# Gates of the last merge with seven products of quarters instead of eight

## The chip, the cores and the metric

The kernel runs on one core of one Trainium2 chip. A core has a matrix unit (TensorE, PE in the profile; its weight loads are shown apart as PEld), three engines that work element by element (VectorE, DVE; ScalarE, ACT; GpSimd, POOL), SyncE (SP), which issues most transfers here, and 16 DMA engines that move data between DRAM and the on-chip memories. SBUF is the large on-chip memory with 128 partitions; PSUM is the small one into which TensorE sums. Each engine takes its own instructions in order and waits on semaphores for the others.

The metric is the time of one execution on the device, in microseconds (us).

## The reference

One layer of a network with three parallel branches, over 2048 sample tokens and 128 prompt tokens, 1024 channels wide, all in float32:

```python
proj = jnp.einsum('btd,de->bte', xn, w_in)            # xn: modulated RMSNorm of x
qkv, beta, dec, z_a, u_b, v_b, z_b, x_c, z_c, gates = jnp.split(proj, points, axis=-1)
# A: short convolution of qkv, gated delta rule in both directions -> o_a   (512 channels)
# B: gating by a spatial matrix in chunks of 128 tokens            -> o_b   (512)
# C: Fourier mixing over tokens and channels                       -> o_c   (512)
br = jnp.stack([o_a, o_b, o_c], axis=2)
pb = jnp.einsum('btnw,nwd->btnd', br, w_branch)       # 512 -> 1024, per branch
gt = jax.nn.sigmoid(gates.reshape(B, T, N_BRANCH, D_MODEL))
merged = jnp.einsum('btnd,btnd->btd', gt, pb)
out = jnp.einsum('btd,de->bte', merged, w_out)
# then y = rmsnorm(x + gate * out)
```

What the change touches is `gates` of branch A: a product of the normalized tokens (2176 x 1024) with 1024 columns of `w_in`, whose sigmoid multiplies branch A's projection.

## The kernel before

**Numbers.** Every float32 operand of a matmul is split into two float16 parts, a high and a low one, and a product is three matmuls: high by high, high by low, low by high. TensorE thus does 3 matmuls for each 128 channels of the inner dimension (`gemm_T`, line 162 calls `mm`, line 161). Before the split an operand is scaled by a power of two that comes from its sum of squares.

**Tiles.** The normalized tokens lie in SBUF for the whole run as two tiles `xh` and `xl` (128 partitions x 8 blocks of channels x 2176 tokens). Tokens are taken in five blocks, four of 512 and one of 128 (`TBS`). A gate row is one block of 128 output channels (`db`); for a block of 512 tokens it costs 8 x 3 = 24 matmuls of 512 columns, and the branch product, with 4 blocks of channels, costs 12.

**Weights.** All weight blocks stand in one list, `wlist`, in the order of use. Each is read by SP into one of two staging buffers (`wst`, `read_w`) and converted there by a generator, `converting`: ScalarE squares it with a running sum (line 209), VectorE casts the sum (line 175), a one-column matmul adds it over partitions, VectorE makes the power of two from it in four small operations (lines 183 to 187) and its inverse (216), ScalarE writes the high part (218), VectorE the low part (219). Conversions are pushed forward by `weight_step`, one step at a time, from inside the matmul loops (`pace.tick`); `getw(n, ahead)` hands out the next blocks and asks for those ahead.

**Stages.** Norms and the input projection of decays and gates for branch A; 12 blocks of the short convolution, each over the five token blocks, beside which the decays of the delta rule are worked out and stored (`decays`, up to about 275 us; later convolutions to 450 us); the preparation of the delta rule with branches B and C; the three merges, for B, C and A in this order (`merge`, lines 1324 to 1374), the scan of the delta rule running beside the first two; then the output projection.

**A merge** runs over 8 rows `db`; in each, over two halves of the tokens and their blocks: gate product, sigmoid with its scale (ScalarE, line 1351), branch product from `big` (branch values in high and low parts), product of the two (VectorE, 1360), addition to the row `mrow` read from DRAM (read by SP, line 1339; addition on GpSimd, 1361; store by GpSimd's queue, 1368). The last merge, for branch A (line 1461), takes the halves in reversed order. In each of its rows `tail` also reads and converts one block of 128 columns of `w_out` (`out_w`) into tiles of their own, `wohi` and `wolo`, and `gate_rows` makes the output gate. After the later tokens of the last row, `ahead_out` prepares the first five output tiles (`out_prep`: square, scale, high part at line 1428, low part); the prompt's tile comes first, then tokens 1024 to 2047, then the others.

**Order.** The instructions of each engine are put in order when the program is built: a planner simulates the engines and places the instructions by their dependences and its own costs; `tc.high_priority()` moves the ones inside ahead. A pool's `bufs` says how many tiles of a name exist, and so when the next can be written.

Of the kernel before, what the change touches and what calls it, by code (L numbers as in the profile page):

```python
# [11 lines left out]
F16 = mybir.dt.float16  # L12
# [25 lines left out]
FS = 4096.0  # L38
TBS = [(0, 512), (512, 512), (1024, 512), (1536, 512), (2048, 128)]
# [72 lines left out]
def hybrid_flow_kernel(ctx: ExitStack, tc: tile.TileContext, x_prompt, x_sample, state_delta, c, c_ctx, ln_g, w_ada,  # L112
# [85 lines left out]
    def converting(w, st, nkt, cols=P, hi=None, lo=None, tag="w", bufs=5):  # L198
# [15 lines left out]
        s, inv = scales(None, wp, "wsc", sb16)  # L214
# [12 lines left out]
    xh = sb(xnp, [P, KT, NTOK], "xh", F16)  # L227
    xl = sb(xnp, [P, KT, NTOK], "xl", F16)

    def gemm_T(ps, w, c0, rh, rl, nkt=KT, start=True, stop=True):  # L230
        for k in range(nkt):
            mm(ps, w.hi[:, k, c0:c0 + P], rh[:, k, :], start and k == 0, False)
            mm(ps, w.hi[:, k, c0:c0 + P], rl[:, k, :], False, False)
            mm(ps, w.lo[:, k, c0:c0 + P], rh[:, k, :], False, stop and k == nkt - 1)
            if k % 2:
                pace.part(rh.shape[-1] / 400)

    def gemm_N(ps, lh, ll, w, c0, n, nkt=KT):
        for k in range(nkt):
            mm(ps, lh[:, k, :], w.hi[:, k, c0:c0 + n], k == 0, False)  # L240
            mm(ps, lh[:, k, :], w.lo[:, k, c0:c0 + n], False, False)
            mm(ps, ll[:, k, :], w.hi[:, k, c0:c0 + n], False, k == nkt - 1)
# [13 lines left out]
    for n in (1, 2, 0):  # L256
        for db in range(KT):
            wlist.append((w_in_[:, C_G + n * D + db * P:C_G + n * D + (db + 1) * P], KT, "w", 4))
            wlist.append((w_branch[0, n][:, db * P:(db + 1) * P], 4, "b", 2))
# [4 lines left out]
    def read_next():  # L264
        if len(wread) < min(len(wdone) - len(wsteps) + 2, len(wlist)):
            src, nkt, tag, bufs = wlist[len(wread)]
            wread.append(read_w(src, nkt))

    def begin():

        i = len(wdone)
        if i >= goal[0] or (wlist[i][2] == "b" and not bwp):
            return False
        if len(wread) == i:
            read_next()
        wdone.append(_W())
        wsteps.append(converting(wdone[i], wread[i], wlist[i][1], tag=wlist[i][2], bufs=wlist[i][3]))
        return True

# [134 lines left out]
    with tc.high_priority():  # L414
# [6 lines left out]
        A.activation(bnd[:, 0, :], ms.rearrange("p k g -> p (k g)"), AF.Square, scale=math.sqrt(2.0 * D), accum_out=bss[:, 0:1])  # L421
        A.activation(bnd[:, 1, :], sh.rearrange("p k g -> p (k g)"), AF.Square, scale=math.sqrt(2.0), accum_out=bss[:, 1:2])
# [15 lines left out]
    for ti, (t0, tn) in enumerate(TBS):  # L438
# [13 lines left out]
        for k in range(KT):  # L452
# [5 lines left out]
            A.copy(xh[:, k, t0:t0 + tn], t)  # L458
            G.tensor_tensor(xl[:, k, t0:t0 + tn], t, xh[:, k, t0:t0 + tn], ALU.subtract)
        for g in range(4):  # L460
            ps = bank(ps_d if tn == P and g % 2 else ps_mm, [P, tn])
            gemm_T(ps, zaw[g], 0, xh[:, :, t0:t0 + tn], xl[:, :, t0:t0 + tn])
# [32 lines left out]
    def decays():  # L495
        pbs = sb(dq, [P, NCH, 16], "sq")
        for c0, c1 in ((0, 9), (9, NCH)):
            pb = bank(ps_mm, [P, c1 - c0, 32])
            for t in range(c0, c1):
                ts = slice(t * P, (t + 1) * P)  # L500
                for k in range(KT):
                    if k == KT - 1:
                        mm(pb[:, t - c0, 0:16], xl[:, k, ts], bdp[:, k, 0:16], False, False)
                    mm(pb[:, t - c0, :], xh[:, k, ts], bdp[:, k, :], k == 0, k == KT - 1)
                    if k < KT - 1:
                        mm(pb[:, t - c0, 0:16], xl[:, k, ts], bdp[:, k, 0:16], False, False)
# [74 lines left out]
        def flush(t, row):  # L581
            A.activation(row, row, AF.Exp)
            A.dma_start(decD[t], row.rearrange("p d h i -> p d (h i)"))
# [20 lines left out]
    flip = [0]  # L604
    pace.start(decays(), 1.2)
    for ct in range(12):
        w = getw(1, 2 if ct < 6 else min(4, 15 - ct))
        for half in range(1):
# [4 lines left out]
            for t0, tn in TBS:  # L613
                flip[0] ^= 1
                ps = bank(ps_d if flip[0] else ps_mm, [P, tn])
                gemm_T(ps, w, 0, xh[:, :, t0:t0 + tn], xl[:, :, t0:t0 + tn])
# [17 lines left out]
    pace.drain()  # L634
    a1.close()
# [467 lines left out]
    def silu_unit(ti, w):  # L1103
        t0, tn = TBS[ti]
        ps = bank(ps_mm, [P, tn])
        gemm_T(ps, w, 0, xh[:, :, t0:t0 + tn], xl[:, :, t0:t0 + tn])
# [48 lines left out]
    for t in range(NCH):  # L1155
        ps = bank(ps_mm, [P, 4, P])
        ts = slice(t * P, (t + 1) * P)
# [370 lines left out]
```

## Time and profile before

| | us |
|---|---|
| median of 3 runs | 2205.78 (2198.61 to 2207.93) |
| the profiled execution | 2208.47, of which the span is 2206.7 |
| TensorE busy | 2138.4 (97% of the span) |
| VectorE / ScalarE / GpSimd busy | 1299.4 / 1005.0 / 708.8 |
| later convolutions | 275 to 450 |
| delta preparation, branches B and C | 450 to 1084 |
| merge B, merge C | 1084 to 1417.9, 1417.9 to 1750.0 |
| merge A (the last) | 1750.0 to 2018.5 |
| output projection | 2018.5 to 2206.7 |

In the views of the profile a line such as `L161 PE MATMUL b<-xh,whi` names the line of the kernel, the engine, the operation, the tile written and those read; x and a number are how many; min/median/max and means of one instruction are in nanoseconds, starts in us from the start of the span. What stands in brackets behind `<-` is what ended the idle time of the engine just before. A helper's line stands for all its callers, so the tile's name tells which it is. Matmuls overlap in TensorE: one of 512 columns is shown as 0.38 us long, but the next one starts 0.216 us later, and the spacing is what counts.

### The profile page before, as it was taken

What the parts mean: (1) busy time and instruction counts of PE and PEld (TensorE: products, weight loads), DVE (VectorE), ACT (ScalarE), POOL (GpSimd) and SP (SyncE); (2) the same over time, 40 slices, a digit from 0 to 9 for tenths busy, and PEclk for the clock granted to TensorE, in tenths of its full rate; (3) what the DMA queues carried; (4) which work ended last, traced back from release to release, by engine and by line L of the source; (5) the groups of instructions that cost most, each with busy time, mean ns of one, the idle gap of its engine ahead of it and who ended that gap; (6) DMA issues with size and microseconds to landing.
All of it is one profiled execution on the core that took longest, in us unless ns stands there. A gap on an engine that the chain in (4) does not pass through costs nothing.

```text
span 2206.7 us, 42033 instructions
## 1 busy us (share of the span) xinstructions
PE 2138.4 (97%) x15966; PEld 1230.7 (56%) x15966; DVE 1299.4 (59%) x3081; ACT 1005.0 (46%) x2322; POOL 708.8 (32%) x860
## 2 busy tenths in 40 slices
PE   7999999999999999899899999899999999999998
PEld 3564444455555588778555565555555444444443
DVE  5736854479869688255665555755574544233454
ACT  3545644455465564344644445655553422222332
POOL 1421333223334322432322223354442222112543
PEclk9999999999999999999999999999999999999999
DMA  8434733277686762433655556766664544333542
GB/s 280 144 94 157 277 98 101 66 214 224 219 245 221 204 187 86 118 116 119 214 178 162 171 158 187 239 185 213 201 204 150 168 124 129 118 101 120 174 149 104
DMA packets 304276, 365.05 MB, mean 165 GB/s; under 512 B 39393, under 2 KB 215626, under 8 KB 302026
## 3 DMA queue, kind: packets, MB, share of 16 engines
q1 hardware_dynamic: 288938, 302.19, 45.3%
q0 software_dynamic: 12688, 51.27, 6.5%
q10 hardware_dynamic: 2448, 8.91, 1.0%
q8 instruction: 125, 2.05, 0.4%
q14 instruction: 77, 0.63, 0.1%
HBM read 234.67 MB, written 127.62 MB: 164 GB/s over the span
## 4 chain that ended last, share of the span: by engine, by line
PE 50%; DMA 6%; DVE 5%; ACT 3%; issue 2%; POOL 1%; SPq 0%; DVEq 0%; POOLq 0%; ACTq 0%
PE b L161 49%; DMA st<-br 1%; DMA wst<-in_w_branch_dram 1%; DVE XB L779 1%; DVE E L780 1%; DMA wst<-in_w_in_dram 1%; DMA XB<-nd 0%; DMA mt<-mrg 0%; ACT of L1032 0%; POOL o L1029 0%; DVE big L1322 0%; DMA mrow<-mrg 0%; DVE wlo L219 0%; ACT big L1321 0%; DMA S<-in_state_delta_dram 0%
## 5 line engine op out<-in xcount | busy, mean ns | idle before, releaser
L161 PE MATMUL b<-xh,whi 128*128 128x512 f16 (+1 forms) x1920 | 651.3, 348 | 4.8 <-DVE vrow L1198 1.7
L161 PE MATMUL b<-xl,whi 128*128 128x512 f16 (+1 forms) x1920 | 652.1, 348 | 0.0
L161 PE MATMUL b<-xh,wlo 128*128 128x512 f16 (+1 forms) x1920 | 651.1, 348 | 0.0
L161 PEld LDWEIGHTS <-whi 128*128 128x128 f16 x3904 | 356.5, 98 | 332.9 <-issue 12.9
L161 PEld LDWEIGHTS <-wlo 128*128 128x128 f16 x1952 | 191.2, 98 | 178.4 <-issue 2.1
L161 PE MATMUL b<-big,bhi 128*128 128x512 f16 (+1 forms) x960 | 250.7, 348 | 1.0 <-DVE big L1322 1.0
L1361 POOL TENSOR_TENSOR mrow<-mrow,sg 128x512 f32<-128x512 f32 (+1 forms) x80 | 94.3, 1179 | 292.9 <-DVE sg L1360 163.8
L161 PE MATMUL b<-big,blo 128*128 128x512 f16 (+1 forms) x480 | 163.3, 347 | 0.0
L1351 ACT ACTIVATE sg<-b,winv 128x512 f32<-128x512 f32 (+1 forms) x120 | 74.1, 618 | 152.2 <-PE b L161 151.8
L161 PEld LDWEIGHTS <-xh 128*128 128x128 f16 x1496 | 117.1, 98 | 29.7 <-issue 1.4
L628 POOL TENSOR_TENSOR cy<-cy,raw 128x545 f32<-128x545 f32 (+1 forms) x48 | 69.8, 1480 | 185.9 <-ACT raw L627 185.9
L161 PEld LDWEIGHTS <-bhi 128*128 128x128 f16 x960 | 87.0, 98 | 75.8 <-issue 0.3
L175 DVE CAST wscb<-wss 128x1 bf16<-128x1 f32 x93 | 14.3, 154 | 186.1 <-ACT wlo L209 84.1
L1360 DVE SCALAR_TENSOR_TENSOR sg<-b,binv,sg 128x512 f32<-128x512 f32 (+1 forms) x80 | 53.5, 668 | 104.5 <-PE b L161 91.3
L848 POOL COPY T<-ES 32x256 f16<-32x256 f16 x68 | 29.4, 432 | 223.0 <-DMA ES<-ei 204.9
L161 PE MATMUL b<-wohi,mh 128*128 128x512 f16 x240 | 91.0, 379 | 2.6 <-ACT mh L1428 2.6
L161 PE MATMUL b<-whi,xl 128*128 128x128 f16 x544 | 92.9, 219 | 0.0
L161 PE MATMUL b<-wlo,xh 128*128 128x128 f16 x544 | 92.9, 219 | 0.0
L161 PE MATMUL b<-whi,xh 128*128 128x128 f16 x544 | 92.9, 219 | 0.0
L219 DVE SCALAR_TENSOR_TENSOR wlo<-wst,wsc,whi 128x1024 f16<-128x1024 f32 x52 | 74.4, 1434 | 28.5 <-ACT whi L218 28.2
L161 PE MATMUL b<-wohi,ml 128*128 128x512 f16 x240 | 90.9, 379 | 0.3 <-DVE mscb L175 0.3
L161 PE MATMUL b<-wolo,mh 128*128 128x512 f16 x240 | 91.0, 379 | 0.0
(449 smaller groups left out, 4283.1 us busy)
## 6 DMA issues: line engine op xcount, KB each, us to landing
wst<-in_w_in_dram SPq DMA_DIRECT2D x60, 512.0 KB, 5.4
qkv<-cy POOLq DMA_DIRECT2D x12, 1089.0 KB, 5.2
st<-br SPq DMA_DIRECT2D x48, 256.0 KB, 5.1
mrow<-mrg SPq DMA_DIRECT2D x18, 512.0 KB, 4.1
mrow<-mrg SPq DMA_DIRECT2D x16, 576.0 KB, 4.4
mrg<-mrow POOLq DMA_DIRECT2D x16, 576.0 KB, 3.6
dc<-dec SPq DMA_DIRECT2D x17, 512.0 KB, 5.2
kq<-qkv SPq DMA_DIRECT2D x34, 256.0 KB, 5.5
```

What stands on the lines that cost most here:

```text
L161: PE.matmul(out, l, r, start=start, stop=stop)
L175: V.tensor_copy(sb16, ss)
L219: V.scalar_tensor_tensor(w.lo, st, s, w.hi, ALU.mult, ALU.subtract)
L628: G.tensor_tensor(y[:, c0:c1], y[:, c0:c1], raw[:, 1 + c0:1 + c1], ALU.mult)
L779: V.tensor_tensor(t3, X3[:, 0:k, k:k + 1].to_broadcast([P, k, n_]), E3[:, k:k + 1, k:32].to_broadcast([P, k, n_]), ALU.mult)
L780: V.tensor_tensor(E3[:, 0:k, k:32], E3[:, 0:k, k:32], t3, ALU.subtract)
L848: G.tensor_copy(T16[rows(a0, b), :, :, b], ES[0:32, :, 2 * a0 + b, :, wT])
L1351: A.activation(sg, ps, AF.Sigmoid, scale=gw.inv)
L1360: V.scalar_tensor_tensor(sg, ps, binv[:, 1:2], sg, ALU.mult, ALU.mult)
L1361: G.tensor_tensor(mr, mr, sg, ALU.add)
```

## The change

**Tokens in quarters.** `xh` and `xl` become four tiles `XQ[a][b]`, 2 MB each with both parts (tokens below 1024 or from 1024 on; channels 0 to 511 or 512 to 1023), and one for the prompt, `xpr`. All products take their operands through `x_all`; their count does not change. In the code `XQ[0]` is `(A21, A22)` and `XQ[1]` is `(A11, A12)`.

**Strassen's method** multiplies two matrices in 2 x 2 blocks by seven products instead of eight, from sums of the blocks. Here (in Winograd's form) the blocks are the token quarters on one side and, on the other, the weight blocks of row `j` and row `4 + j`, each in its upper and lower 512 channels.

**Token sums** (`token_sums`): S1 = A21 + A22, S2 = S1 - A11, S3 = A11 - A21, S4 = A12 - S2, in pieces of 512 tokens by 128 channels, each split into high and low parts and stored in DRAM (`sD[0]`, `sD[1]`, `sD[2]`, `sD[3]`, 2 MB each). They are worked out in the convolution stage, after the last transfer of the decays.

**Weight sums** (`summed`): where a round of the last merge needs a sum of two or four weight blocks, the second block is read into `wax`, the first into `wtx`, GpSimd adds or subtracts, and the result is converted as usual (`converting_sum`). `read_next` lets one more read stand open for sums than before.

**The last merge** (`last_merge`) has four rounds of four rows `j`:
1. tokens from 1024 on, and prompt: row `j` by its own two halves of channels, the first kept in `U[j]`, the second added to it before the sigmoid. Meanwhile `sD[1]` is read into the tile of A21.
2. `sD[1]` by the sum "t2" (512 channels only); the result is added to `U[j]`. In its first row the reads of `sD[0]` and `sD[3]` into the tiles of A11 and A12 are issued.
3. the sums "t1": `sD[0]` gives `M5[j]`, then `sD[3]` finishes row `4 + j` of the later tokens. `sD[2]` is read into A21's tile.
4. the sums "t3": `sD[2]` finishes row `4 + j`, and A22 row `j`, of the earlier tokens; branch products of both.

The prompt's tokens take part with their own channel halves. The sum of a partial result with a kept one is a VectorE operation (`plus`), after which ScalarE takes the sigmoid of the sum (`shut`); before, ScalarE read the product from PSUM with its scale.

**Output weights** are converted in round 4 (1, 2, 3 and 2 blocks in its rows, `OW`), into the tiles of A11 and A12, which are free by then. The tiles of the first five output tiles come from `U`, `M5`, `wtx` and `wax`; they are prepared in the last row of round 4.

```diff
-    xh = sb(xnp, [P, KT, NTOK], "xh", F16)
-    xl = sb(xnp, [P, KT, NTOK], "xl", F16)
+    XQ = [[sb(xnp, [P, 2, 4, 1024], f"x{a}{b}", F16) for b in range(2)] for a in range(2)]
+    xpr = sb(xnp, [P, 2, KT, NP], "xp", F16)
...
+    for j in range(4):
+        wlist += [(gw_(0, j), KT, "w", 4), bw_(0, j)]
+    wlist += [(gw_(0, 4 + j), 4, ("t2", j), 4) for j in range(4)]
+    for j in range(4):
+        wlist += [(gw_(0, 4 + j), KT, ("t1", j), 4), bw_(0, 4 + j)]
+    for j in range(4):
+        outs = [(w_out[0][:, i * P:(i + 1) * P], KT, "o", i) for i in range(KT)]
+        wlist += [(gw_(0, 4 + j), KT, ("t3", j), 4)] + outs[OW[j][0]:OW[j][1]] + [bw_(0, 4 + j), bw_(0, j)]
...
+    def summed(i, st):
+        kind, ax = wlist[i][2][0], taux[i]
+        a, b = st[:, 0:4], st[:, 4:8]
+        if kind == "t1":
+            G.tensor_tensor(a, a, ax[:, 0:4], ALU.subtract)
+            return st
...
+            sums_ = i in TS
+            if sum((q in TS) == sums_ for q in range(len(wdone) - len(wsteps), i)) > 1:
+                return
+            if sums_:
+                st = sb(upp[0], [P, KT, P], "wtx", bufs=2)
+                SY.dma_start(st, src.rearrange("(k p) c -> p k c", p=P))
...
+        for tb in (0, 512):
+            for k in range(4):
+                x21, x22 = whole(k, tb), whole(4 + k, tb)
+                V.tensor_tensor(x22, x21, x22, ALU.add)
+                pair_out(0, x22, k, tb, V)
+                yield 1
+                x11 = whole(k, 1024 + tb)
+                G.tensor_tensor(x21, x11, x21, ALU.subtract)
+                pair_out(2, x21, k, tb, V)
+                yield 1
...
     pace.drain()
+    with tc.issue_after(dlast[0].ins):
+        for _ in sums:
+            pass
...
+        SY.dma_start(A21, sD[1])
+        for j in range(4):
+            w, bw = getw(2, 2)
+            bi, mr = scaled(bw), row(j, 1024, 1152)
+            for t0, tn in T1_:
+                ps = bank(ps_mm, [P, tn])
+                gemm_T(ps, w, at1(A11, t0, tn) if t0 < NS else pr(0))
+                with tc.high_priority():
+                    A.activation(U[j][:, t0 - 1024:t0 - 1024 + tn], ps, AF.Copy, scale=w.inv)
+                work()
...
+        for j in range(4):
+            w = getw(1, 2)
...
+                gemm_T(ps, w, at1(A21, t0, tn) if t0 < NS else pr(0))
+                u_ = U[j][:, t0 - 1024:t0 - 1024 + tn]
+                plus(u_, ps, w.inv if t0 < NS else ninv, u_)
+                work(2)
+            next(gates, 0)
+            if j == 0:
+                SY.dma_start(A11, sD[0])
+                SY.dma_start(A12, sD[3])
...
+        for j in range(4):
+            w = getw(1, 5)
+            m2 = row(4 + j, 0, 1024)
+            s2, s1 = [], []
+            for t0, tn in T2_:
+                ps = bank(ps_mm, [P, tn])
+                gemm_T(ps, w, nkc(A21, t0, tn))
+                s2.append(shut(M5[j][:, t0:t0 + tn], ps, w))
+                u_ = U[j][:, t0:t0 + tn]
+                plus(u_, ps, w.inv, u_)
+                work(3)
+            out_inv_w(j)
+            b2, b1 = getw(2, 5)
+            i2, i1 = scaled(b2), scaled(b1)
+            for i, (t0, tn) in enumerate(T2_):
+                ps = bank(ps_mm, [P, tn])
+                gemm_T(ps, w, nkc(A22, t0, tn), 4)
+                s1.append(shut(U[j][:, t0:t0 + tn], ps, w))
+                work(3)
+                product(b2, i2, s2[i], m2[:, t0:t0 + tn], t0, tn)
+                work(2)
...
-    merge(0, False, inv_, tail, HALVES[::-1], ahead_out)
+    last_merge(0, inv_)
```

More of the change, by code (lines that the diff above doesn't have):

```diff
@@ L38 @@
 FS = 4096.0
+OW = [(0, 1), (1, 3), (3, 6), (6, 8)]
 TBS = [(0, 512), (512, 512), (1024, 512), (1536, 512), (2048, 128)]
@@ L213, in converting @@
             yield
-        s, inv = scales(None, wp, "wsc", sb16)
+        if wnext[0] < 16:
+            s, inv = scales(None, wp, "wsc", sb16)
+        else:
+            with tc.high_priority():
+                s, inv = scales(None, wp, "wsc", sb16)
         w.inv = sb(wp, [P, 1], "winv", bufs=10)
@@ L1439, in half_gate @@
         gp.append(t)
-    def ahead_out(h0):
-        if h0:
-            for i, t in enumerate(order[:5]):
-                pre.append(out_prep(t, *((wp, "wst") if i % 3 else (big, "mrow")), None if i < 3 else wp))
-            for i in range(2):
-                half_gate(i)
-                scale_gate(gp[i], gp[i], pre[0][2][:, 4 * i:4 * i + 4])
     def scale_gate(out, src, inv):
```

298 lines of the change are left out of this document (231 added, 67 removed).

## The prediction, made before the result was known

> **What bounds the kernel now.** I read the page's busy shares first, then a table of busy time by stage, then the chain that ended last, then TensorE's own timeline.
>
> ```profile
> PE 2138.4 (97%) x15966; PEld 1230.7 (56%) x15966; DVE 1299.4 (59%) x3081; ACT 1005.0 (46%) x2322; POOL 708.8 (32%) x860
> ```
>
> ```profile
> 275.00:450.00 175.00, 175.00 (x948) 84.79 (x946) 83.78 (x119) 76.60 (x121) 52.08 (x69) 1.00 0.29 95
> 450.00:1084.00 634.00, 608.77 (x5481) 422.00 (x5479) 460.34 (x1190) 326.59 (x926) 206.72 (x277) 0.99 0.59 178
> 1084.00:1417.90 333.90, 322.70 (x2931) 192.24 (x2929) 202.09 (x530) 166.96 (x399) 91.71 (x141) 1.00 0.60 185
> 1417.90:1750.00 332.10, 326.87 (x2652) 187.65 (x2652) 190.74 (x503) 167.82 (x460) 139.09 (x161) 1.00 0.62 190
> 1750.00:2018.50 268.50, 268.50 (x1480) 130.02 (x1477) 97.23 (x272) 73.06 (x120) 55.58 (x58) 1.00 0.38 117
> 2018.50:2206.70 188.20, 177.13 (x833) 80.05 (x831) 91.54 (x184) 55.55 (x82) 82.62 (x70) 0.99 0.43 143
> ```
>
> Columns: stretch, length, busy time of PE, PEld, DVE, ACT, POOL, granted clock, DMA share, GB/s. The rows are the later convolutions, delta preparation with branches B and C, three merges' stretches (the last merge is 1750 to 2018.5), and the output stage. TensorE is the bound throughout; in the last merge it is busy for all 268.5 us while DVE is at 36%.
>
> ```profile
> 1697.05 306.04 PE b L161 x1706
> ...
> 2045.33 153.28 PE b L161 x720
> ```
>
> The chain is matmuls alone through the whole last merge: a matmul removed there shortens the run by its own pitch, as long as nothing else is late. The pitch is in the timeline.
>
> ```profile
> 1747.99 0.22 PE L161 MATMUL b<-xh,whi 128*128 128x128 f16 x1
> ...
> 1749.33 0.28 PE L161 MATMUL b<-big,bhi 128*128 128x128 f16 x2
> ...
> 1750.03 0.38 PE L161 MATMUL b<-xh,whi 128*128 128x512 f16 x1
> ...
> 1755.21 0.59 PE L161 MATMUL b<-big,bhi 128*128 128x512 f16 x2
> ...
> 2018.48 0.17 PE L161 MATMUL b<-mscb,ones 128*128 128x1 bf16 x1
> 2021.23 0.39 PE L161 MATMUL b<-wohi,mh 128*128 128x512 f16 x1 [2.59 <-ACT mh L1428]
> ```
>
> 24 matmuls of 512 columns take 1755.21 - 1750.03 = 5.18 us, 0.216 us each; 24 of 128 columns take 1749.33 - 1747.99 = 1.34 us, 0.056 each. The last row is the only idle time at the hand-over to the output stage.
>
> The profiled execution took 2208.47 us (span 2206.7 and 1.8 around it); the median of the runs is 2205.78, so I take 2.7 off my sum at the end.
>
> **Part 1, products removed.** Before: 8 rows of gates x 4 blocks x 24 = 768 matmuls of 512 columns. After, in four rounds of four rows: round 1 (row j by its own halves) 4 x 2 x 24 = 192, round 2 (two summed quarters) 4 x 2 x 12 = 96, round 3 192, round 4 192: 672. The prompt's 128 columns keep 192 (24 + 12 + 12 a row in pairs of rows), the branch products 384. So 96 fewer: -96 x 0.216 = -20.7 us. The rounds then last, if TensorE never waits: 4 x (72 x 0.216 + 36 x 0.056) = 70; 4 x 5.85 = 23.4; 4 x 16.9 = 67.6; 4 x 96 x 0.216 = 82.9.
>
> **Part 2, token sums in the convolution stage.** For each of 8 pairs of row and half-block: 4 widenings, one subtraction and one low part on POOL, 6 operations on DVE, 4 copies on ACT, 4 stores on SP.
>
> ```profile
> L459 POOL TENSOR_TENSOR xl<-xm,xh 128x512 f16<-128x512 f32 x32 | 41.6, 1318 | 52.8 <-ACT xh L458 52.8
> L458 ACT CAST xh<-xm 128x512 f16<-128x512 f32 x32 | 19.2, 613 | 17.6 <-DVE xm L457 17.2
> L1360 DVE SCALAR_TENSOR_TENSOR sg<-b,binv,sg 128x512 f32<-128x512 f32 x64 | 47.9, 749 | 97.8 <-PE b L161 88.8 <-issue 4.9 <-ACT sg L1351 3.7
> ```
>
> POOL 48 x 1.32 = 63 us, DVE 48 x 0.75 = 36, ACT 32 x 0.61 = 20, and 32 x 256 KB of stores. From 275 to 450 us POOL is free for 123 us, DVE 91, ACT 98, and the DMA share is 0.29. In the changed order these instructions stand between the convolutions, after the decay rows. On SP the weight reads stand behind stores that wait for ACT and DVE, but one weight is wanted every 4 x 5.2 + 1.3 = 22 us. I take 0. If the cover failed, a delay of PSUM copies behind one POOL-contended operation, some 3 us, is the top; a gain is excluded, since nothing is taken away there.
>
> **Part 3, sums read back.** Four loads of 2 MB replace x in its own tiles. The first has 70 us. The two for round 3 can start only when round 1 is done with these tiles, and are wanted 23.4 us and 28.6 us later.
>
> ```profile
> xt<-in_x_sample_dram SPq DMA_DIRECT2D x4, 2048.0 KB, 12.8
> ...
> wst<-in_w_branch_dram SPq DMA_DIRECT2D x24, 256.0 KB, 2.8
> ...
> wst<-in_w_out_dram SPq DMA_DIRECT2D x8, 512.0 KB, 4.6
> ```
>
> Two in series take 25.6 us: they just fit. But SP is one queue, and round 3's first weights stand behind them; each then waits 4.6 us for its landing, 1.3 for POOL's subtraction and 1.25 for the square (1.06 and 0.19 for its sum's read, rows in part 4) before its scale matmul, which stands in TensorE's queue ahead of the rest of round 2. Everything behind that small matmul waits with it. 0 if the loads keep the row's pace, 6 if a weight load follows both; I take 2, nearer 0, as the planner put the small matmuls late in the round. POOL's subtraction queues ahead of the merge additions, which nothing on TensorE waits for.
>
> **Part 4, weight supply in round 4.** This is the part that decides. Before, three weights were converted in each row of 33 us. The output weights now go into x's own tiles, which are free only after round 3, so round 4 converts 8 output weights, 8 branch weights and 4 sums, 20 in 82.9 us, through the same two staging buffers (sums have two of their own). Prices:
>
> ```profile
> L219 DVE SCALAR_TENSOR_TENSOR wolo<-wst,wsc,wohi 128x1024 f16<-128x1024 f32 x8 | 10.2, 1281 | 6.3 <-ACT wohi L218 6.2
> L218 ACT ACTIVATE wohi<-wst,wsc 128x1024 f16<-128x1024 f32 x8 | 9.1, 1141 | 7.1 <-DVE wsc L186 7.1
> L219 DVE SCALAR_TENSOR_TENSOR blo<-wst,wsc,bhi 128x512 f16<-128x512 f32 x8 | 6.0, 750 | 0.0
> L218 ACT ACTIVATE bhi<-wst,wsc 128x512 f16<-128x512 f32 x8 | 5.8, 720 | 22.1 <-DVE wsc L186 18.9 <-DVE wsc L187 3.2
> L183 DVE COPY wsc<-b 128x1 f32<-128x1 f32 x23 | 3.4, 151 | 8.5 <-PE b L161 8.5
> ```
>
> ```profile
> L209 ACT ACTIVATE zlo<-wst x4: 1054/1056/1057, 39.0 to 56.8; 128x1024 f16<-128x1024 f32 x4
> L209 ACT ACTIVATE blo<-wst x24: 629/630/633, 1051.4 to 1971.3; 128x512 f16<-128x512 f32 x24
> L209 ACT ACTIVATION_READ_ACCUMULATOR wolo<-wst x8: 186/186/188, 1761.1 to 1978.0; 128x1 f32 x8
> ```
>
> DVE first: 40 evictions (three additions and two products for each of 8 blocks) x 0.75 = 30.0; low parts 10 x 1.28 + 7 x 0.75 = 18.1 (three weights are ready earlier); 17 chains of six small operations at 0.15 = 15.3; the output's first tiles some 6. That is 69 of 82.9 us, 84%, where it was 36%. It is not over full, so the question is the chain: load, square, cast, small matmul, scales, high part, low part. The only row with large weights converted back to back through two buffers is the first: four squares from 39.0 to 56.8, 5.9 us apiece. A branch weight is (0.63 + 0.72 + 0.75) / (1.06 + 1.14 + 1.28) = 0.60 of that, 3.6. Eight of each: 47 + 29 = 76 us, under 82.9, no stall: the low end. With the four sums in the same line, 4 x 5.9 more, 99.6: 16.7 late, the high end. I take 8, the middle: the sums have buffers of their own but the same engines. The built order points the same way: in the third and fourth rows of round 4 TensorE has the first two matmuls of two branch products ahead of the third of either, which makes sense only where the low part comes late. ACT also squares the output stage's first tiles between weights, and there waits for their loads, with weights queued behind.
>
> **Part 5, hand-over and other stages.** 2.6 us idle stand at the hand-over now; five tiles are again prepared ahead, so 0, between -2.6 and +4. From the convolutions on, the planner's order of other engines' work is not the same as before; TensorE's idle time in the rows from 450 to 1750 is 25.2 + 11.2 + 5.2 = 42 us, and a tenth of it either way is 4. I take 0.
>
> Sum: 2208.5 - 20.7 + 0 + 2 + 8 + 0 = 2197.8, less 2.7: 2195.
>
> **Rivals.**
> A. *Nothing is late*: parts 3 and 4 at their low ends, 2205.8 - 20.7 = 2185. For it: DVE at 84% and the order was planned for this. Against: SP, ACT and DVE run in order and round 4 has 20 small matmuls in TensorE's queue. 0.18.
>
> B. *Slower: conversions go one at a time.* Each weight's chain runs end to end, because ACT stands before a load or DVE before the part in front.
>
> ```profile
> 1960.23 1.06 ACT L209 ACTIVATE wolo<-wst 128x1024 f16<-128x1024 f32 x1 [1.93 <-DMA wst<-in_w_out_dram]
> ```
>
> ```profile
> 1967.17 1.28 DVE L219 SCALAR_TENSOR_TENSOR wolo<-wst,wsc,wohi 128x1024 f16<-128x1024 f32 x1 [1.47 <-ACT wohi L218]
> ```
>
> One output weight took 8.2 us from square to low part. 12 x 8.2 + 8 x 4.9 = 138, less three ready ones, 20: 118 against 82.9, so +35, and 2205.8 - 20.7 + 35 = 2220. It decides from 21 us of stalls in round 4 on; slower by 0.5% takes 32. Against it: in the first stage two buffers gave 5.9, not 8.2. 0.20.
>
> C. *A few long waits that also slow the clock*: round 3 starts late by 6 and round 4 loses its 16.7; 2205.8 - 20.7 + 6 + 16.7 = 2208, with half of round 4's loss 2199.
>
> ```profile
> 875.00:900.00 25.00, 18.94 (x115) 12.99 (x114) 12.30 (x24) 9.22 (x18) 7.24 (x9) 0.93 0.63 146
> 900.00:925.00 25.00, 25.00 (x309) 22.22 (x309) 5.95 (x14) 8.94 (x23) 12.59 (x18) 0.93 0.27 87
> ```
>
> Here 6.1 us idle go with a granted clock of 0.93 over 50 us, 3.5 us more; the 2.6 us at the hand-over left it near full. So only waits beyond some 3 us cost twice. 0.20.
> The Trainium skill ("TensorE: Matmul & The Clock Gate", Part 1) says that an idle window of about 3.4 us halves the array's clock until a busy window has passed, and advises no idle gaps over about 3 us. By that rule each long wait costs up to 1.7 us beside itself, and four of them would put the sum near 2202; the two rows agree in sign and are larger.
>
> That the change does less than it says is out: the built kernel has 96 fewer 512-column matmuls.
>
> **Chances.** My forecast, waits of 4 to 15 us, 0.42; C 0.20; B 0.20; A 0.18. Faster by 0.5%, which is about what a measurement can tell here, means below 2194.8: A and half of the forecast lie there (0.39), C and the other half within the bound (0.41), B and its surroundings above 2216.8 (0.20). Range: A's 2184 at the bottom; at the top C's 2208, part 5's 4 and the lower half of B, 2218.
>
> **What would show it.** Right: convolutions (275 to 450) still without TensorE idle; the last merge at some 255 us with 8 to 12 us idle, most of it in its last 90 us before branch products whose releaser is a low part on DVE, or before small matmuls. DVE over 80% there. Wrong: an idle last merge of over 20 us (B), none (A), a wait of several us for the tiles of x between rounds 2 and 3 (C), or a changed idle sum between 450 and 1750 of more than 5 us, which nothing here foresees.

## The result, and the profile after

The changed kernel takes 2256.37 us (median of 4 runs, 2253.22 to 2256.66), the kernel before 2206.26 beside it: a ratio of 1.0231, with a 95% interval of 1.0205 to 1.0256. I had forecast 2195 and a range up to 2218. The change is 2.3% slower, and a stage to which I had given zero lost 48.5 us.

Busy shares of the changed kernel's page, and its busy time by stage (stretch, length, PE, PEld, DVE, ACT, POOL, granted clock, DMA share, GB/s). The stretches end at the same events as those shown of before:

```profile
PE 2135.3 (95%) x15886; PEld 1229.9 (55%) x15886; DVE 1435.4 (64%) x3329; ACT 1054.4 (47%) x2416; POOL 841.5 (37%) x940
```

```profile
275.00:498.50 223.50, 183.40 (x939) 87.14 (x937) 143.26 (x164) 96.06 (x154) 129.25 (x111) 0.91 0.34 115
498.50:1126.30 627.80, 606.35 (x5482) 423.96 (x5480) 460.56 (x1193) 327.93 (x927) 206.52 (x277) 0.99 0.59 180
1126.30:1458.50 332.20, 324.76 (x2950) 193.57 (x2948) 202.03 (x530) 168.23 (x402) 92.90 (x141) 1.00 0.61 187
1458.50:1789.40 330.90, 324.91 (x2640) 186.44 (x2639) 197.40 (x514) 169.73 (x461) 143.15 (x164) 1.00 0.66 205
1789.40:2067.70 278.30, 258.35 (x1393) 123.50 (x1393) 167.41 (x465) 104.46 (x184) 92.56 (x87) 0.97 0.53 166
2067.70:2254.30 186.60, 176.68 (x831) 79.92 (x828) 89.36 (x177) 50.84 (x76) 82.06 (x69) 0.99 0.41 138
```

Row by row against before: the convolutions are 48.5 us longer (223.5 for 175.0), the next three stages together 9.1 us shorter (6.2, 1.7 and 1.2), the last merge 9.8 longer (278.3 for 268.5) although it has 96 matmuls less, the output stage 1.6 shorter. That is 47.6, the difference of the spans. There are two losses, then: the convolutions, where the token sums now stand, take some 48 us more, and the last merge takes 30.5 us more than its matmuls need (247.8, the 268.5 of before less 20.7).

**The convolutions.** What TensorE waited for between 275 and 500 us (releaser: sum, times, longest; in the kernel before, the view of 275 to 450 us, the same stretch, is empty):

```profile
PE b L162 <- DVE wscb L176: 30.3, 3, 15.1
PE b L162 <- ACT raw L740: 9.8, 5, 3.2
```

`wscb` is the cast in front of the one-column matmul of a weight's scale. `raw` is the copy of a convolution's PSUM result, and a late copy keeps a PSUM bank. 40.1 us of idle are in these eight waits. In the other 8.4 us TensorE was busy longer with the same matmuls (183.4 us for 175.0), at a granted clock of 0.91 in the row above.

The longest wait, 15.05 us, followed back through the timeline (start, duration, instruction, idle time before it and its releaser):

```profile
368.74 0.56 SPq L196 DMA_DIRECT2D wst<-in_w_in_dram  x1
...
380.90 2.70 POOL L749 TENSOR_TENSOR cy<-cy,raw 128x545 f32<-128x545 f32 x2
383.57 2.13 POOL L694 TENSOR_TENSOR st<-sg,st 128x512 f16<-128x512 f32 x1
385.66 1.26 POOL L712 TENSOR_TENSOR sg<-sg,sg 128x512 f32<-128x512 f32 x1
...
386.95 0.62 ACT L693 CAST st<-sg 128x512 f16<-128x512 f32 x1 [3.83 <-POOL sg L712]
...
388.31 1.05 ACT L210 ACTIVATE wlo<-wst 128x1024 f16<-128x1024 f32 x1
...
389.23 1.34 DVE L743 TENSOR_SCALAR cy<-raw,pc 128x2178 f32<-128x2178 f32 x1
390.49 0.68 DVE L719 TENSOR_TENSOR sg<-sg,sg 128x512 f32<-128x512 f32 x1
391.09 0.14 DVE L176 CAST wscb<-wss 128x1 bf16<-128x1 f32 x1
...
391.29 0.16 PE L162 MATMUL b<-wscb,ones 128*128 128x1 bf16 x1 [15.05 <-DVE wscb L176]
```

The weight was asked for at 368.74. Its square starts at 388.31, behind casts of the sums on ACT, and one of these waits 3.83 us for POOL, where the sum's subtraction stands behind a low part and two products of the convolution. The cast then stands behind a convolution's and a sum's operation on DVE. No engine is full. But a conversion passes SP, ACT, DVE and TensorE one after the other, and each does its own work in order. On the first three, work of the sums stood in front of it, and ACT's part of that work was itself waiting for POOL.

The operations of the sums also took longer than I had priced them: from 275 us on, the stage has 59.5 us more work on DVE than before (143.3 for 83.8; 36 were forecast), 77.2 more on POOL (129.3 for 52.1; 63 were forecast) and 19.5 more on ACT (20 were forecast). Durations as minimum/median/maximum in ns:

```profile
L694 DVE TENSOR_TENSOR st<-sg,st x24: 677/1602/3267, 270.0 to 393.6; 128x512 f16<-128x512 f32 x24
L694 POOL TENSOR_TENSOR st<-sg,st x8: 1147/1515/3469, 278.8 to 393.2; 128x512 f16<-128x512 f32 x8
L702 POOL TENSOR_TENSOR sg<-x x32: 1147/1538/3334, 153.0 to 387.6; 128x512 f32<-128x512 f16 x32
```

**The last merge.** What TensorE waited for in rounds 1 to 3 (the first fence, 1789.4 to 1965) and in round 4 (the second, 1965 to 2067.7), and the busy time of the two stretches:

```profile
PE b L162 <- DVE wscb L176: 8.6, 4, 3.4
PE b L162 <- DVE sg L1486: 1.2, 1, 1.2
```

```profile
PE b L162 <- ACT bhi L223: 4.3, 3, 2.8
PE b L162 <- DVE blo L224: 2.7, 2, 2.2
PE b L162 <- DVE wsc L186: 2.1, 2, 1.7
PE b L162 <- DVE wscb L176: 1.0, 2, 0.8
PE b L162 <- DVE wsc L188: 0.8, 1, 0.8
```

```profile
1789.40:1965.00 175.60, 167.00 (x969) 83.51 (x969) 99.07 (x267) 55.15 (x104) 58.48 (x58) 0.98 0.54 169
1965.00:2067.70 102.70, 91.35 (x428) 40.00 (x425) 68.34 (x199) 49.32 (x81) 34.08 (x29) 0.95 0.52 162
```

Rounds 1 to 3 take 175.6 us where their matmuls need 161.0, round 4 takes 102.7 where they need 82.9. (The rounds of the prediction leave out the small matmuls of the scales and the gate: their sum is 243.9, 3.9 short of 247.8.) All waits but that of 1.2 us for `sg`, at the stage's edge, end with a step of a weight conversion, as forecast. But TensorE was idle for 20.0 us (278.3 less 258.4) where 10 were forecast, and at a granted clock of 0.97 it was also busy for 10.6 us more than 247.8: 30.5 in all.

### The profile page after: what moved, and what is told of

It reads as the page before. It is cut to its first block, busy times and chain, and to the rows that moved or that the text cites. A ratio compares the mean times of both kernels' runs of the same rounds, so it can differ in the third digit from the quotient of the medians.

```text
span 2254.3 us, 42521 instructions
## 1 busy us (share of the span) xinstructions
PE 2135.3 (95%) x15886; PEld 1229.9 (55%) x15886; DVE 1435.4 (64%) x3329; ACT 1054.4 (47%) x2416; POOL 841.5 (37%) x940
## 5 line engine op out<-in xcount | busy, mean ns | idle before, releaser
L162 PE MATMUL b<-x,whi 128*128 128x512 f16 x3008 | 907.5, 382 | 9.4 <-ACT raw L740 6.2
L162 PE MATMUL b<-x,wlo 128*128 128x512 f16 x1504 | 573.9, 382 | 0.0
L162 PEld LDWEIGHTS <-x 128*128 128x128 f16 x2176 | 131.3, 98 | 41.5 <-issue 1.4
L162 PE MATMUL b<-x,m 128*128 128x512 f16 x528 | 115.0, 379 | 0.0
L176 DVE CAST wscb<-wss 128x1 bf16<-128x1 f32 x109 | 16.7, 153 | 127.9 <-ACT wlo L210 66.8
L162 PE MATMUL b<-whi,x 128*128 128x128 f16 x1024 | 90.7, 219 | 0.0
L162 PE MATMUL b<-wlo,x 128*128 128x128 f16 x512 | 87.4, 219 | 0.0
L162 PEld LDWEIGHTS <-m 128*128 128x128 f16 x528 | 50.9, 98 | 63.1 <-issue 2.0
L210 ACT ACTIVATE wlo<-wst 128x1024 f16<-128x1024 f32 x48 | 50.7, 1057 | 67.4 <-DMA wst<-in_w_in_dram 64.4
L162 PE MATMUL b<-xp,whi 128*128 128x128 f16 x768 | 75.0, 223 | 4.0 <-ACT raw L740 4.0
L162 PE MATMUL b<-x,zhi 128*128 128x512 f16 x256 | 77.9, 380 | 0.7 <-POOL x L540 0.7
L162 PE MATMUL b<-v4hi,x 128*128 128x512 f16 x256 | 77.1, 379 | 0.0
```

The source lines that it names most:

```text
L162: PE.matmul(out, l, r, start=start, stop=stop)
L176: V.tensor_copy(sb16, ss)
L210: A.activation(w.lo, st, AF.Square, accum_out=ss)
```

## The experiments

The length of the convolutions is taken from the first start of a PSUM copy to the last (160.4 to 426.9 before, 158.2 to 475.4 in the changed kernel: 266.5 and 317.2 us). All ratios are to the kernel before on the same chip. The results stand in this table; the readings follow. Each stage length is that of one execution, the profiled one; the four runs in which the convolutions and the sums are as in the changed kernel gave 310.0 to 318.2 us, so a difference of 8 us there says nothing.

| run | us | ratio (95%) | convolutions |
|---|---|---|---|
| changed kernel | 2256.37 | 1.0231 (1.0205 to 1.0256) | 317.2 |
| no sums | 2211.25 | 1.0023 (1.0011 to 1.0035) | 266.6 |
| sums on the kernel before | 2253.67 | 1.0201 (1.0176 to 1.0226) | 316.5 |
| sums not stored | 2256.59 | 1.0224 (1.0207 to 1.0241) | 311.2 |
| sums without POOL | 2244.65 | 1.0161 (1.0141 to 1.0182) | 293.3 |
| the same, not stored | 2243.54 | 1.0171 (1.0143 to 1.0198) | 294.5 |
| late convolutions reuse a weight | 2257.09 | 1.0228 (1.0201 to 1.0255) | 290.2 |
| no output weights | 2244.35 | 1.0181 (1.0161 to 1.0200) | 318.2 |
| sums not read back | 2254.52 | 1.0222 (1.0186 to 1.0259) | 310.0 |
| the merge's products alone | 2188.11 | 0.9910 (0.9893 to 0.9928) | 266.5 |
| sums in merges B and C | 2230.07 | 1.0107 (1.0085 to 1.0129) | 266.5 |
| branch weights first | 2273.25 | 1.0296 (1.0270 to 1.0322) | 316.7 |
| the last two together | 2239.94 | 1.0146 (1.0124 to 1.0167) | 266.5 |

**Are the convolutions' 48 us the sums?** One run leaves them out, one adds them to the kernel before.

```diff
-    with tc.issue_after(dlast[0].ins):
-        for _ in sums:
-            pass
+    for i_, (a_, b_) in enumerate([(0, 0), (0, 1), (1, 0), (1, 1)]):
+        SY.dma_start(sD[i_], XQ[a_][b_])
```

> The changed kernel without the token sums: the four sums are not computed, and four plain stores of 2 MB put the unsummed quarters of x in their places (the gates of the last merge are then of wrong operands). Theory: the 48.5 us by which the convolutions end later are the sums' work on POOL, DVE, ACT and SP. Then the convolutions end within 3 us of the kernel before, and the run takes 2208 us, or up to 2217 if the stages between (9 us shorter in the changed kernel) go back to their old length. Rival: the stage is slowed by the layout of x in quarters or by the 8 MB written; then it stays above 2240 us.

```diff
 (the kernel before)
+    sD = [dram(f"xs{i}", [P, 2, 4, 1024], F16) for i in range(4)]
+    sums = token_sums()          # from xh and xl
...
     pace.drain()
+    with tc.issue_after(dlast[0].ins):
+        for _ in sums:
+            pass
```

> The kernel before, with the token sums computed and stored as in the changed kernel, and not used. Theory (the sums alone do it): the convolutions end 40 to 50 us later, 2245 to 2255 us. Rival (it takes the changed layout of x or the changed order of the rest): less than 10 us later, under 2216 us.

Without them the stretch from 275 us on has no idle TensorE (row of the run without sums), and the kernel before gets the same waits as the changed one (its waits between 270 and 500 us):

```profile
275.00:450.00 175.00, 175.00 (x947) 84.80 (x946) 82.29 (x119) 77.44 (x122) 52.14 (x69) 1.00 0.28 92
```

```profile
PE b L161 <- DVE wscb L175: 30.3, 3, 13.9
PE b L161 <- ACT raw L660: 10.7, 6, 3.4
```

So the sums alone do it, 45 to 47 us, and neither the quarters of x nor the 8 MB written, which the run without sums also writes, have a part in it. That run also says that the rest of the change is no gain: 2211.25, 0.2% above before. Its last merge takes 279.0 us, 10.5 more than before; the stages between the convolutions and that merge are 9.1 us shorter than before (627.3 + 663.6 for 634.0 + 666.0), as in the changed kernel. That shortening therefore comes with the change itself and not with the sums.

**By which path: SyncE's queue, POOL, or the order on the engines?**

```diff
-            if owed:
-                SY.dma_start(*owed.pop())
-            owed.append((sD[i][:, :, k, tb:tb + 512], o))
...
-        SY.dma_start(*owed.pop())
...
+    for i_, (a_, b_) in enumerate([(0, 0), (0, 1), (1, 0), (1, 1)]):
+        SY.dma_start(sD[i_], XQ[a_][b_])
```

> The changed kernel with all sums computed, but without their 32 stores; four plain stores at the end of the stage put unsummed quarters of x in their places. Theory Q (SyncE's queue: reads of weights stand behind stores that wait for the sums): the convolutions lose under 12 us instead of 48, 2208 to 2220 us. Theory E (DVE, ACT and POOL, each in order: weight conversions and PSUM copies stand behind operations of the sums): they still lose 30 us or more, 2238 to 2256 us.

```diff
-            G.tensor_tensor(t_, h_, l_, ALU.add)
+            V.tensor_tensor(t_, h_, l_, ALU.add)
...
-                G.tensor_tensor(x21, x11, x21, ALU.subtract)
+                V.tensor_tensor(x21, x11, x21, ALU.subtract)
...
-                pair_out(3, x12, k, tb, G)
+                pair_out(3, x12, k, tb, V)
```

> The changed kernel with the 48 operations of the sums that run on POOL moved to DVE. If the wait is for POOL (its operations took 1.78 us in the mean beside DVE's, and ACT's casts wait for them in order), the convolutions lose 10 to 25 us instead of 48, 2218 to 2233 us. If the wait is for SyncE's queue, or for the sheer number of operations, they lose 40 or more, 2248 us or above.

> All sums on DVE, as in the run without POOL, and without their 32 stores (four plain stores at the end). In that run ACT's casts waited 27.4 us for stores out of the three buffers. If these waits carry the 27 us that the convolutions still lost, they lose under 8 us here: 2217 to 2226 us. If it is the order on DVE and ACT itself (the sums ahead of the casts and scales of weights), they still lose 18 us or more: 2235 us or above.

(The last is the edits of both.) Without the stores the stage is 6 us shorter, no more than it varies by itself, and the time is the same: SyncE's queue is not the cause. Without POOL's part the stage loses 26.8 us instead of 50.7, about half. The total fell by less (2244.65) than to the 2218 to 2233 expected; the profiled execution, from which the stage is read, was the fastest of its four (2237.94). Taking the stores away there as well changes nothing, so ACT's 27.4 us of waits for store buffers were not on the path either. What TensorE still waits for between 270 and 420 us in the run without POOL:

```profile
PE b L162 <- DVE wscb L176: 20.3, 3, 7.0
```

Three conversions, each some 7 us late (19.7 us in three waits in the run without stores too); the waits for PSUM copies are gone with POOL's part. Why half of the work on POOL makes the loss twice as large shows in the duration of the same low part without it:

```profile
L694 DVE TENSOR_TENSOR st<-sg,st x32: 675/682/1571, 265.4 to 372.4; 128x512 f16<-128x512 f32 x32
```

0.68 us in the median, where it was 1.60. Counted in the timelines of both engines, of the changed kernel's DVE additions and subtractions of 512 columns between 275 and 395 us 34 overlapped one of POOL (0.68 to 3.27 us, median 1.62) and 5 did not (0.67 to 0.69). Summed up over the traces, all 96 operations took DVE 77 us where it had them alone; in the changed kernel, half of them took DVE 60 us and the other half took POOL 84.

**Do the sums act through the weight conversions alone?**

```diff
-    for c0 in ([C_QKV + i * P for i in range(12)] + [C_V + g * P for g in range(4)]
+    for c0 in ([C_QKV + i * P for i in range(7)] + [C_V + g * P for g in range(4)]
...
-        w = getw(1, 2 if ct < 6 else min(4, 15 - ct))
+        if ct < 7:
+            w = getw(1, 2 if ct < 5 else 6 - ct)
```

> The changed kernel with convolution blocks 7 to 11 done with block 6's weights: five weight blocks less are read and converted while the sums are worked out, and none ahead for the next stage (which then begins later, so the stage is read from the trace, from the first PSUM copy of the convolutions to the last; 266.5 us in the kernel before, 317.2 in the changed one). Theory: the sums delay TensorE through the conversions (their scale matmul stands in its queue): the stage loses 10 us or less, the waits for PSUM copies, 277 us. Rival: the sums also hold up the PSUM copies and the convolutions' own work, and these waits take the place of the others: 295 us or more.

(Blocks 7 to 11 of the convolution multiply by block 6's weights.) The stage took 290.2 us, neither of the two. With no conversion to wait for, TensorE's waits between 275 and 420 us were

```profile
PE b L162 <- ACT raw L741: 18.5, 7, 6.0
```

So the sums have a second way to TensorE: 23.7 of the 50.7 us remain, in waits for PSUM copies, which stand on ACT behind casts of the sums. In the changed kernel these waits are 9.8 us; here they take the place of the others in part. Before the two longest (6.0 and 4.0 us) ACT had waited 6.5 and 6.4 us for a store to free its buffer, so here the stores seem to lie on the path. The run also takes five weights' own work off ACT and DVE, so its share for the conversions is, if anything, too large. The total is no lower, since the next stage's weights were not ready (14.1 us of waits for two scales behind the stage); the stage alone is to be read here.

**What the last merge loses.** One run converts no output weights, one does not read the sums back, and one leaves out both and the sums themselves.

```diff
-        wlist += [(gw_(0, 4 + j), KT, ("t3", j), 4)] + outs[OW[j][0]:OW[j][1]] + [bw_(0, 4 + j), bw_(0, j)]
+        wlist += [(gw_(0, 4 + j), KT, ("t3", j), 4)] + [bw_(0, 4 + j), bw_(0, j)]
...
-            V.tensor_mul(winv[:, i:i + 1], getw(1, 3).inv, sx)
+            V.tensor_mul(winv[:, i:i + 1], wout[2], sx)
```

> The changed kernel without the 8 output weight blocks: they are not read and not converted (the output stage multiplies by what lies in those tiles). Round 4 then converts 12 blocks instead of 20. Theory: the last merge's 22 us of idle and the clock lost with it come from the weight supply of round 4. Then it shortens by 20 to 28 us, to 2228 to 2236 us. Rival: the waits come from the sums read back, and from ScalarE and VectorE in front of the branch products; then it shortens by under 8 us, to 2248 or more.

```diff
-        SY.dma_start(A21, sD[1])
...
-            if j == 0:
-                SY.dma_start(A11, sD[0])
-                SY.dma_start(A12, sD[3])
...
-            if j == 0:
-                SY.dma_start(A21, sD[2])
```

> The changed kernel without the four loads of 2 MB that bring the token sums into the tiles of x in the last merge (the sums' gates are then of the unsummed quarters). Theory: the first three rounds lose 9 us in four waits of 1.8 to 3.4 us, and these loads on SyncE's queue are their cause: 5 to 10 us shorter, 2246 to 2251 us. If the waits there are for in-order ScalarE and VectorE, under 3 us shorter.

> The changed kernel without the token sums, without their loads in the last merge and without the output weights: what the seven products bring when only they are left. By the count 96 matmuls less, 20.7 us, with waits of some 5 us left in the first three rounds: 2188 to 2195 us. If waits of VectorE and ScalarE in the last merge take the place of the removed ones, 2200 or more.

Rows of the last merge in the run without output weights, the run without reads (with its waits for scales from 1780 to 1960 us), and the one without all three:

```profile
1795.20:2056.90 261.70, 252.78 (x1386) 122.86 (x1386) 154.64 (x418) 88.29 (x161) 89.78 (x87) 0.98 0.51 160
```

```profile
1780.08:2053.30 273.22, 255.70 (x1394) 121.58 (x1394) 165.95 (x465) 103.47 (x182) 89.99 (x86) 0.98 0.48 146
```

```profile
PE b L162 <- DVE wscb L176: 4.8, 4, 2.9
```

```profile
1746.26:2001.90 255.64, 248.63 (x1387) 120.97 (x1387) 153.41 (x418) 88.02 (x161) 87.63 (x87) 1.00 0.47 139
```

278.3 us become 261.7 without output weights (all waits of round 4 are gone, 16.6 us), 273.2 without the reads (5.1), and 255.6 without either. The totals fell by less than the theories said: by 12 us in the first run, between theory (20 to 28) and rival (under 8), and by 2 in the second, whose runs (2243.6 to 2260.4) lie too far apart to decide between 5 to 10 and under 3. The last run, 2188.11 as expected, is 0.9% below before: it is the only one that is faster, and it leaves work out. In its last merge TensorE is busy for 248.6 us at a clock of 1.00, so the 96 matmuls are worth what they should be; 7 us of waits are left. That stage is 12.9 us shorter than before; the rest of the run's gain lies in other stages.

**Can the sums and the conversions stand elsewhere?** Two changes of order that compute everything, and both together.

```diff
+        for tb in (0, 256, 512, 768):     # 16 groups of 12 DVE operations on 256 tokens
+            for k in range(4):
...
+                    V.tensor_tensor(v, *x_at(k_, t0, 256), ALU.add)
...
                     pace.tick(tn * MT)
+                    if (n, db) in SUMROWS and t0 in SUMROWS[n, db]:
+                        next(sums, 0)
```

> The changed kernel with the token sums moved from the convolutions to the merges of B and C: all operations of the sums on DVE, in 16 groups of 12 operations on 256 tokens, one group in every second or third token block from row 1 of merge B to row 3 of merge C (some 450 us instead of 120). Theory (the convolutions lose because the sums stand too densely among the steps of weight conversions): the merges lose under 10 us, 2211 to 2221 us, where 2211 is the run without sums. Rival (each operation added to DVE delays a conversion, wherever it stands): the merges lose 20 us or more, over 2230 us.

```diff
-... [(gw_(0, 4 + j), KT, ("t3", j), 4)] + outs[OW[j][0]:OW[j][1]] + [bw_(0, 4 + j), bw_(0, j)]
+... [(gw_(0, 4 + j), KT, ("t3", j), 4)] + [bw_(0, 4 + j), bw_(0, j)] + outs[OW[j][0]:OW[j][1]]
...
-            out_inv_w(j)
-            b2, b1 = getw(2, 5)
+            b2, b1 = getw(2, 5)
...
             m1 = row(j, 0, 1024)
+            out_inv_w(j)
```

> The changed kernel with round 4's weights in another order: each row's two branch weights are converted before its output weights, and the output weights are asked for only after the first two branch products. Theory (round 4's waits of 2.2 to 2.8 us before branch products are conversions that stand behind output weights): 6 to 12 us shorter, 2244 to 2250 us. Rival (20 conversions are too many for the stage in any order): the wait moves to the weight sums of the next row, within 4 us of 2256.

> Both together: sums in the merges of B and C, branch weights before output weights in round 4. If both theories hold, 2200 to 2215 us, and below the kernel before (2206) only if the merges lose under 5 us; if neither, 2240 or more.

Spread over merges B and C the sums cost 19 us (2230.07 against 2211.25), not 45. That is nearer to the rival, which had 20 us or more and over 2230, than to the theory with under 10. The two merges, with the sums and without them:

```profile
1079.00:1418.00 339.00, 325.22 (x2914) 191.83 (x2912) 252.97 (x670) 181.69 (x441) 101.24 (x140) 1.00 0.65 198
1418.00:1759.60 341.60, 327.18 (x2671) 189.40 (x2669) 223.94 (x567) 178.08 (x487) 145.21 (x165) 0.99 0.67 208
```

```profile
1079.00:1414.00 335.00, 326.59 (x2964) 194.57 (x2963) 202.92 (x532) 168.58 (x404) 94.35 (x141) 1.00 0.62 186
1414.00:1742.60 328.60, 323.53 (x2635) 185.83 (x2631) 197.40 (x513) 169.37 (x459) 141.78 (x164) 1.00 0.67 206
```

680.6 us against 663.6, in many waits of up to 3.6 us, none of them for the scale of a weight: here other short chains of these stages come late. DVE goes from 60% to 70% busy, and that is already felt. The other order in round 4 made the run 17 us slower, where the theory had 6 to 12 us faster and the rival no more than 4 either way. Of the 16.1 us between the profiled executions, 6.6 lie ahead of the last merge, where the edit changes nothing; the merge takes 280.4 us (2.1 more) and the output stage 194.0 (7.4 more). The waits went to the next row's sum of weights, as the rival said, and to the hand-over. These are TensorE's waits from 1980 to 2090 us there:

```profile
PE b L162 <- DVE wscb L176: 8.4, 4, 4.8
PE b L162 <- ACT whi L223: 6.4, 2, 5.5
PE b L162 <- DVE msc L184: 3.0, 1, 3.0
PE b L162 <- ACT m L1547: 2.3, 1, 2.3
```

Both changes together took 2239.94 us, at the edge of the 2240 that stood for neither theory. No version that computes everything beat the kernel before.

## Why the prediction was wrong

*Part 1, right.* -20.7 us for 96 matmuls: in the run with the merge's products alone, the last merge has 248.6 us of work where the sum had 247.8. That this whole run is 19.5 us below before, close to 20.7, is luck: its last merge is 12.9 us shorter, and other stages, which part 1 does not touch, give the rest.

*Part 2 is the step that failed.* "I take 0", with 3 us at the top: the sums cost 45 us. The work was more than forecast, 59.5 us on DVE and 77.2 on POOL for 36 and 63, but it still fitted into the free time counted there (91 and 123). Between 275 and 400 us no engine is full, in the changed kernel (the first row) as in the run without sums (the second):

```profile
275.00:400.00 125.00, 84.90 (x405) 39.28 (x403) 100.32 (x100) 54.91 (x91) 101.11 (x76) 0.84 0.38 130
```

```profile
275.00:400.00 125.00, 125.00 (x677) 60.44 (x676) 63.67 (x93) 59.72 (x92) 40.05 (x56) 1.00 0.29 95
```

DVE is busy for 100 of 125 us and POOL for 101, and yet TensorE gets through 405 matmuls where it did 677. What failed is the step from free time to cover: I compared each engine's free time with the work and called the rest cover. The steps named as harmless in that part were the ones that hurt. "One weight is wanted every 22 us" is true, but its conversion, whose chain has no slack beside an engine that is 80% busy, waited 20 us from its read to its square. And the top of the range, one late PSUM copy, took one wait where there were eight. I looked at SyncE's queue, which didn't matter, and not at ACT, DVE and POOL, which run in order too.

A second error in it, smaller, is the one that made the work longer: 0.75 us for a DVE operation came from a row with one operand in PSUM (the product of L1360). The sums' operations have both in SBUF and took 1.62 us beside POOL, 0.68 without (medians); the 48 of them took 1.26 in the mean. The Trainium skill ("SBUF — State Buffer", Who interferes with whom, and the Summary behind it) says that a DVE instruction with two SBUF inputs contends with a GpSimd instruction that reads SBUF, and that the second one to issue waits until the first is done. The 34 and 5 operations above agree with it, and so does the run without POOL, where half the stage's loss is gone.

*Parts 3 and 4: the mechanism was right, the sizes too small.* Rounds 1 to 3 waited 8.6 us for scales (2 were taken, 6 at the top). Without the loads 4.8 us are left, so the loads make some 4 to 5 us, within the range of part 3; the other waits for scales had no term in the sum. Round 4 lost 19.8 us by the rounds' count (8 taken, 16.7 at the top), of which 10.9 are waits, all at branch products and scale matmuls as named, though more often for the high part on ACT than for the low part on DVE; without the output weights they are gone. DVE's busy time in round 4 was 68.3 us, 69 were forecast, but in 102.7 us: 67%, not 84%. The clock had no price in either part: the last merge has five stretches of 3.4 us at half of the full clock (the last section shows two of them), which is up to 8.5 us of work lost beside 20.0 us of idle.

*Part 5.* The output stage is 1.6 us shorter. The stages between are 9.1 us shorter than before, where I had set 4 either way, and TensorE's idle time there is 34.9 us where it was 41.6, a change of over 5 us, which I had named as a sign of being wrong. The run without sums shows the same 9.1, so it is the changed order or layout; which of them, no run tells.

*Rivals.* C, at 2208, is near the run without sums (2211.25), and it named what the last merge shows, waits that also slow the clock. But the closeness of the numbers is luck: C had 22.7 us of loss in the last merge, where 30.5 were lost, and the 9.1 us won in the stages between were in no part. B named the right object, conversions that come late one after another, but in the wrong stage. No rival had the convolutions in it, so no range could reach 2256.

*Still open:* that POOL's half of the sums hurts through the PSUM copies and DVE's half through the conversions is read from the waits, and not taken apart further. No run gave conversions precedence over the sums on DVE and ACT, so the order on the engines is what the timeline shows and not what a run has proved.

## What to carry to other kernels

Free time of an engine is cover only for work that nobody waits for. Where a chain of short steps passes the same in-order engines (here ten steps on four engines for each weight), added work delays every step, and with two engines 80% busy the chain came up to 15 us late, though none was full. Look for the most latency-bound chain in the stage, count the queues that it shares with the added work, and price the stall from there; take the price of an operation from a row with its operands in the same memory and with the same neighbour busy.

## What the runs showed of the hardware

Two engines slow each other. A VectorE operation of 512 columns with both inputs in SBUF took 0.68 us alone and 1.62 beside GpSimd (medians), whose own operations went from 1.15 to as much as 3.5 us.

Waits of 1 to 3 us that follow one another cost clock as well. In round 4 of the changed kernel (timeline of TensorE; a wait of 0.56 us at 2025.64 is left out):

```profile
2023.61 1.47 PE L162 MATMUL b<-big,bhi 128*128 128x512 f16 x4 [2.83 <-ACT bhi L223]
...
2032.79 0.16 PE L162 MATMUL b<-wscb,ones 128*128 128x1 bf16 x1 [1.73 <-DVE wsc L186]
2033.79 1.41 PE L162 MATMUL b<-big,bhi 128*128 128x512 f16 x4 [0.84 <-ACT bhi L223]
```

The granted clock is not a little lower throughout. It is full, or half for a stretch of 3.41 us, and the changes in a trace lie whole multiples of 3.41 us apart. Two such stretches of the changed kernel, each with the one ahead of it (columns as above, the granted clock is the third number from the end):

```profile
2020.67:2024.08 3.41, 0.58 (x4) 0.23 (x4) 3.10 (x15) 2.28 (x3) 0.00 (x0) 1.00 0.41 142
2024.08:2027.49 3.41, 2.85 (x8) 0.83 (x7) 1.51 (x3) 0.73 (x2) 0.00 (x0) 0.50 0.58 156
2030.91:2034.32 3.41, 0.84 (x7) 0.38 (x6) 2.44 (x15) 2.46 (x4) 2.29 (x3) 1.00 0.01 2
2034.32:2037.73 3.41, 3.41 (x10) 1.22 (x9) 2.41 (x9) 1.60 (x2) 0.00 (x0) 0.50 0.95 273
```

In the first, TensorE was busy for 0.58 us beside the wait of 2.83; in the third, for 0.84 us beside the two of 1.73 and 0.84. Behind each, the clock was half for 3.41 us. So several short waits count together when they fall into one such step. The wait of 2.6 us at the hand-over of the kernel before fell across two steps, and the clock stayed full:

```profile
2016.27:2019.69 3.42, 2.38 (x12) 0.98 (x10) 0.54 (x4) 2.42 (x5) 2.03 (x2) 1.00 0.14 36
2019.69:2023.10 3.41, 1.59 (x8) 0.72 (x9) 2.63 (x8) 1.49 (x3) 0.00 (x0) 1.00 0.00 0
```

Counted over the 14 traces in such steps, all 123 at full clock in which TensorE was busy for less than 40% were followed by one at half clock, and none with more than 60%. The Trainium skill ("TensorE: Matmul & The Clock Gate", Part 1) puts the half clock behind an idle window of about 3.4 us. The length agrees; but here the step need not be idle throughout, and no wait in it was 3.4 us long. Where the two differ, the traces decide: C's bound of some 3 us for a wait that costs twice is too high.
